# Four DMA transposes of an encoder kernel replaced by TensorE transposes into PSUM

## The chip, the cores and the metric

The kernel runs on one core of one Trainium2 chip. The metric is the time of one execution in device microseconds (us). The engines are TensorE (PE, with its weight loads PEld), VectorE (DVE), ScalarE (ACT), GpSimd (POOL) and SyncE (SP, which issues most of the transfers).

## The reference, cut to what matters

One encoder layer is applied to two requests (prompt and sample) of 2048 tokens and 1024 features each, with the same weights. Four groups of 256 features are computed side by side, each is multiplied by its own gate, and the concatenation goes through an output projection:

```python
hx = rms_norm(x, pre_g)
proj = hx @ w_in                                     # 1024 -> 12 * 256 + 16 columns
y_a = fourier_mix(a_u, w_fnet) * silu(a_z)           # FNet
y_b = gdn_branch(b_qkv, b_gates, ...) * silu(b_z)    # gated delta rule, both directions
y_c = neighbourhood_attn(cq, ck, cv, rpb) * silu(c_z)
y_d = memory_attn(d_q, rms_norm(mem, mem_g), w_mem_kv) * silu(d_z)
out = concatenate([y_a, y_b, y_c, y_d], -1) @ w_out
return x + rms_norm(out, post_g)
# gdn_branch: q, k, v = split(silu(centred_dwconv(qkv, conv_w)))   5 taps, 4 heads of 64
#   then per chunk of 64 tokens: a triangular solve, and a scan over 32 chunks:
v_new = u_i - w_i @ state
o = qd_i @ state + qk_i @ v_new
state = state * gl_i + kd_i.T @ v_new
# neighbourhood_attn: 32 x 64 grid of tokens, 8 x 16 keys each, softmax with a bias table
# memory_attn: 256 memory tokens, 4 heads, softmax
```

## The kernel before, in words

All large products are made from fp16 parts: a float32 value is split into a high half (the value rounded to fp16) and a low half (the rest), and three matmuls per product stand at lines L464 to L466, L474 to L476 and L480 to L482 (`mm_feat`, `mm_tok`, `mm3`). An operand with tokens on the partitions must be transposed where the features or keys are summed over, and this happens in four places by a DMA on SP's queue:

- `xblock` (L428): 256 rows of x are normalized, split (L446 on ACT, L213 on DVE: tile `xh`) and transposed to `xT` (L448), 16 blocks of 128x128 per instruction. It runs 36 times in `pass_a`, memory tokens included; a copy of `xT` is stored as `xTd` (L531), which the later passes load.
- `conv_pair` and `gdn_conv` (L857, L928): convolution and SiLU of q, k and v of 256 tokens by features, tile `cacc`. v is split into `vt` (L878 on ACT, L227 on POOL) and transposed to `vr` (L937), 16 times.
- `mem_attn.scores` (L1407): the probabilities of 128 tokens over 4 heads and 256 memory tokens are split to `mP` (L1434 on DVE, L227 on POOL) and transposed to `mPT` (L1437), 32 times.
- `na_attn.scores` (L1515): for a pair of tiles of queries the scores `nS` are made (L1561), the probabilities are put into padded tiles `np` as fp16 parts (L1578 on ACT, L1579 on DVE) and transposed to `nPT` (L1582), 64 times.

The stages are traced in this order. `pass_a` projects q, k, v and the gates of the delta rule (a block of 256 tokens at a time); `pass_b` and `pass_z` project what the other groups and the output gates need. `gdn_pre` prepares the delta rule by blocks of 256 tokens (its products are the tiles `lt` and `mt`, L990). `gdn_sub` solves the triangular systems. `gdn_chain` is the scan: 32 steps for each of the two requests, each step one state `S` (L1188 to L1194) that the next step needs. `fnet`, `mem_attn` and `na_attn` (NA) are the other groups. `pass_o` is the output projection of 16 blocks of 256 tokens, each in four quarters of 48 matmuls (`po`, L738 and following) with an `oo` (L748) each; the scale of a block's fp16 parts takes the largest value of a tile through DRAM and back (L331 and L333, tile `p2d`; DVE waits for it in L334).

What sets the order is a scheduler that orders each engine's instructions by a simulated timeline when the kernel is built. Every stage has a band of priorities, lower first: projections and `pass_o` 0, `gdn_sub` and `gdn_chain` 1 (loading a step's operands 1.5), FNet, memory attention and NA 2, `gdn_pre` 3, and the matmuls of the projections 5, so that they fill what the others leave free. Memory orders more: the pools of the left stack are opened one after the other (FNet, memory attention, NA, then the pool of `pass_o`), and those of the right stack too (`gdn_pre`, `gdn_sub`, `gdn_chain`). The PSUM pool `pat` has three tags, `s`, `t` and `o`, with one buffer each (`PSS = ("s", "t")`, `PSV = ("o", "o")`); FNet, memory attention and NA use them in turn, and `pass_o` uses `t`.

## Time and profile before

| | |
|---|---|
| time, median of 3 runs | 2710.26 us (2707.71 to 2711.54) |
| span of the profiled execution | 2710.9 us |
| instructions | 60616 |
| PE busy | 2054.5 us (76%) |
| DVE busy | 2015.0 us (74%) |
| POOL busy | 1130.4 us (42%) |
| ACT busy | 1047.5 us (39%) |
| DMA | 478.35 MB, mean 176 GB/s |

The profile shows one execution. The span is the time from its first to its last instruction on the chip; the profiled execution has no other time of its own on record, and its span lies within the range of the timed runs. Busy time is summed over the span, register and semaphore instructions are left out. The views used below are the page's chain (followed back from the last instruction to what released each step), busy time by window with the granted TensorE clock as a share of full speed, instructions by source line, the timeline of an engine, and waits.

### The profile page before, as it was taken

The page shows a single profiled execution, that of the slowest core. Times are in us where ns is not written, and L with a number is a line of the kernel's source. Part 1 is how long each engine was busy: PE and PEld are TensorE (multiplying, and loading weights), DVE is VectorE, ACT ScalarE, POOL GpSimd, SP SyncE. Part 2 cuts the span into 40 slices and gives each one's busy share as a digit, 9 for nine tenths or more (in the row PEclk, how much of TensorE's full clock was granted, in tenths as well). Part 3 has the DMA queues.
Part 4 walks back from the last instruction along what each step waited for, and adds up shares of the span by engine and source line. Part 5 has one row for each costly group of instructions (what it writes and reads, how often), then busy time and mean ns, then how long its engine had stood idle before and what let it go on. Part 6 is the DMA issues. An engine that isn't in the chain of part 4 may idle for free.

```text
span 2710.9 us, 60616 instructions
## 1 busy us (share of the span) xinstructions
PE 2054.5 (76%) x23664; PEld 1730.0 (64%) x23664; DVE 2015.0 (74%) x4958; ACT 1047.5 (39%) x2544; POOL 1130.4 (42%) x1275
## 2 busy tenths in 40 slices
PE   0676787777667777997589988777788687787778
PEld 0465666666446666775467777667677576676667
DVE  2369988989899979479758758867766567766654
ACT  1345446443454322342254526555542332222221
POOL 1126646455576676427565242222223434433320
PEclk9888888898779898998789989999999888889989
DMA  9799899999956693899489979999997556566443
GB/s 76 150 195 204 192 221 238 213 201 216 171 137 174 200 179 89 202 197 147 114 162 187 186 206 213 204 202 200 192 203 238 141 166 182 142 174 172 142 120 109
DMA packets 834976, 478.35 MB, mean 176 GB/s; under 512 B 562048, under 2 KB 795392, under 8 KB 826240
## 3 DMA queue, kind: packets, MB, share of 16 engines
q1 hardware_dynamic: 810112, 440.92, 76.1%
q10 hardware_dynamic: 24576, 33.56, 4.3%
q8 instruction: 185, 3.03, 0.5%
q14 instruction: 103, 0.84, 0.1%
HBM read 245.60 MB, written 163.75 MB: 151 GB/s over the span
## 4 chain that ended last, share of the span: by engine, by line
DVE 35%; DMA 32%; PE 16%; issue 6%; POOL 4%; SPq 3%; ACT 3%; ACTq 0%; DVEq 0%; POOLq 0%
DMA p2d<-ty 7%; DVE cacc L868 5%; DMA ty<-p2d 3%; DMA nPT<-np__3176_28761 3%; PE pj L464 3%; PE pj L465 3%; PE pj L466 3%; DMA xT<-xh 2%; DMA nPT<-np__3178_28765 2%; DVE pr L1033 2%; DVE T L1036 2%; DMA nPT<-np__3175_28759 1%; DVE ty L243 1%; DMA L<-lt 1%; DVE ty L244 1%
## 5 line engine op out<-in xcount | busy, mean ns | idle before, releaser
L464 PE MATMUL pj<-xT,w 128*128 128x256 f16 x2592 | 744.7, 287 | 140.2 <-DMA xT<-xh 62.7
L466 PE MATMUL pj<-xT,w 128*128 128x256 f16 x2592 | 743.2, 287 | 4.6 <-POOL w L401 4.6
L465 PE MATMUL pj<-xT,w 128*128 128x256 f16 x2592 | 744.2, 287 | 0.0
L464 PEld LDWEIGHTS <-w 128*128 128x128 f16 x2592 | 266.6, 103 | 129.0 <-issue 70.9
L465 PEld LDWEIGHTS <-w 128*128 128x128 f16 x2592 | 266.2, 103 | 104.8 <-issue 62.6
L480 PE MATMUL po<-w,oy 128*128 128x256 f16 x1024 | 292.3, 285 | 15.9 <-DVE oo L748 8.8
L466 PEld LDWEIGHTS <-w 128*128 128x128 f16 x2592 | 266.9, 103 | 56.0 <-issue 6.7
L481 PE MATMUL po<-w,oy 128*128 128x256 f16 x1024 | 292.7, 286 | 0.3 <-issue 0.3
L482 PE MATMUL po<-w,oy 128*128 128x256 f16 x1024 | 292.4, 286 | 0.0
L868 DVE SCALAR_TENSOR_TENSOR cacc<-craw,cws,cacc 128x256 f32<-128x256 f32 x384 | 236.1, 650 | 9.5 <-ACT cacc L866 8.8
L474 PE MATMUL pj<-w,xT 128*128 128x272 f16 (+1 forms) x512 | 153.2, 300 | 50.1 <-ACT st L541 30.6
L475 PE MATMUL pj<-w,xT 128*128 128x272 f16 (+1 forms) x512 | 153.0, 299 | 5.8 <-POOL w L401 5.8
L401 POOL TENSOR_TENSOR w<-wt,w 128x512 f16<-128x512 f32 (+1 forms) x70 | 87.7, 1261 | 161.6 <-ACT w L399 130.9
L476 PE MATMUL pj<-w,xT 128*128 128x272 f16 (+1 forms) x512 | 152.5, 298 | 0.0
L227 POOL TENSOR_TENSOR km<-kt,km 128x256 f16<-128x256 f32 x128 | 105.5, 848 | 110.1 <-ACT km L986 108.6
L1128 POOL COPY bk<-rA 64x512 f16<-64x512 f16 x124 | 79.8, 644 | 159.1 <-DMA rA<-recs 119.0
L480 PEld LDWEIGHTS <-b 128*128 128x128 f16 x1008 | 98.3, 102 | 71.6 <-DVE ct L1179 32.1
L334 DVE TENSOR_REDUCE ty<-ty 128x1 f32<-128x128 f32 x34 | 9.6, 283 | 180.7 <-DMA ty<-p2d 180.7
L227 POOL TENSOR_TENSOR mP<-mP,mP 128x1024 f16<-128x1024 f32 x32 | 68.4, 2137 | 176.7 <-DVE ty L1450 107.7
L1138 POOL COPY b<-cT 64x256 f16<-64x256 f16 x128 | 60.5, 472 | 169.9 <-PE pc L482 161.1
L480 PE MATMUL pno<-nPT,nv 128*128 128x64 f16 x704 | 78.7, 200 | 62.0 <-DMA nPT<-np__3176_28761 24.9
L481 PEld LDWEIGHTS <-oy 128*128 128x128 f16 x1024 | 104.9, 102 | 32.0 <-issue 16.6
(431 smaller groups left out, 6751.0 us busy)
## 6 DMA issues: line engine op xcount, KB each, us to landing
xT<-xTd SPq DMA_DIRECT2D x32, 1024.0 KB
rec<-km SPq DMA_DIRECT2D x32, 768.0 KB
rA<-rec SPq DMA_DIRECT2D x64, 384.0 KB
xTd<-xT SPq DMA_DIRECT2D x16, 1024.0 KB
sz<-st ACTq DMA_DIRECT2D x64, 256.0 KB
oz<-sz SPq DMA_DIRECT2D x16, 1024.0 KB
out_dram<-oo SPq DMA_DIRECT2D x32, 512.0 KB
craw<-braw SPq DMA_DIRECT2D x48, 260.0 KB
```

What stands on the lines that cost most here:

```text
L227: self.nc.gpsimd.tensor_tensor(out=out, in0=a, in1=b, op=ALU.subtract)
L401: eng.tensor_tensor(out=w[:, kk, 1, :], in0=t, in1=w[:, kk, 0, :], op=ALU.subtract)
L464: nc.tensor.matmul(ps, whi, xhi, start=(kt == 0), stop=False)
L465: nc.tensor.matmul(ps, whi, xlo, start=False, stop=False)
L466: nc.tensor.matmul(ps, wlo, xhi, start=False, stop=(kt == KT - 1))
L474: nc.tensor.matmul(ps, xhi, whi, start=(kt == 0), stop=False)
L475: nc.tensor.matmul(ps, xhi, wlo, start=False, stop=False)
L476: nc.tensor.matmul(ps, xlo, whi, start=False, stop=(kt == KT - 1))
L480: nc.tensor.matmul(ps, whi, xhi, start=start, stop=False)
L481: nc.tensor.matmul(ps, whi, xlo, start=False, stop=False)
L482: nc.tensor.matmul(ps, wlo, xhi, start=False, stop=stop)
L868: nc.vector.scalar_tensor_tensor(out=acc[:, f], in0=raw[:, f, t:t + CB], scalar=w[:, t:t + 1], in1=acc[:, f], op0=ALU.mult, op1=ALU.add)
```

## The change

The four DMA transposes are taken out. In their places each 128x128 block is transposed by TensorE (a matmul with an identity) into a tile of `pat`. In `xblock` the two fp16 halves are transposed as they are (eight blocks each, tags `s` and `t`) and copied by ACT to `xT`. In the other three the float32 values are transposed, and the split is made from PSUM: ACT copies the high half to fp16 and DVE subtracts it for the low half. The convolution of v is written to `cacc` in the order of chunks, so that a block of 128 columns holds both feature halves of 64 tokens. NA's padded tiles become float32 without halves, its scores use tag `s` alone (they used `s` and `t` in turn) and its transposes tag `t`. The rest of the diff removes comments and is not shown.

```diff
@@ -445,7 +445,11 @@
...
             self.split_lo(nc.vector, hl[:, 1], xts[t], hl[:, 0], rs[:, t:t + 1])
-            nc.sync.dma_start(dst[:, :, :, t * P:t * P + P].rearrange("p l k t -> p (l k) t"), hl.rearrange("p l c -> p (l c)"), transpose=True)
+            for l in range(2):
+                pt = self.pat.tile([P, KT, P], F16, name=self.nm("pxt"), tag=PSS[l])
+                for k in range(KT):
+                    nc.tensor.transpose(pt[:, k], hl[:, l, k * P:k * P + P], self.ident16)
+                nc.scalar.activation(dst[:, l, :, t * P:t * P + P], pt, AF.Copy)
             self.pace = hl[:, 1, 0:1]
@@ -855,35 +859,45 @@
...
         nc.sync.dma_start(raw, self.D[f"braw{r}"][:, 2 * i:2 * i + 2, tb * CB:tb * CB + CB + 4])
-        acc = pp.tile([P, 2, CB], F32, name=self.nm("cacc"), tag="cacc", bufs=2)
+        acc = pp.tile([P, 2 * CB], F32, name=self.nm("cacc"), tag="cacc", bufs=2)
+        ch = lambda t: t.rearrange("p (n c) -> p n c", c=64)
+        if u == "v":
+            af = [acc.rearrange("p (n f c) -> p f n c", f=2, c=64)[:, f] for f in range(2)]
+        else:
+            af = [ch(acc[:, f * CB:f * CB + CB]) for f in range(2)]
         for f in range(2):
             w = self.cws[:, 2 * i + f]
-            nc.scalar.activation(acc[:, f], raw[:, f, 0:CB], AF.Copy, scale=w[:, 0:1])
+            nc.scalar.activation(af[f], ch(raw[:, f, 0:CB]), AF.Copy, scale=w[:, 0:1])
             for t in range(1, 5):
-                nc.vector.scalar_tensor_tensor(out=acc[:, f], in0=raw[:, f, t:t + CB], scalar=w[:, t:t + 1], in1=acc[:, f], op0=ALU.mult, op1=ALU.add)
-        e = pp.tile([P, 2, CB], F32, name=self.nm("cexp"), tag="cexp", bufs=2)
+                nc.vector.scalar_tensor_tensor(out=af[f], in0=ch(raw[:, f, t:t + CB]), scalar=w[:, t:t + 1], in1=af[f], op0=ALU.mult, op1=ALU.add)
+        e = pp.tile([P, 2 * CB], F32, name=self.nm("cexp"), tag="cexp", bufs=2)
         nc.scalar.activation(e, acc, AF.Tanh, scale=self.cinv[:, i:i + 1])
...
         if u == "v":
-            dst = [self.vt[:, :, l].rearrange("p n f c -> p f n c") for l in range(2)]
+            pv = self.pat.tile([P, CB // 64, P], F32, name=self.nm("pvt"), tag=PSV[0])
+            for n in range(CB // 64):
+                nc.tensor.transpose(pv[:, n], acc[:, n * P:n * P + P], self.ident)
+            nc.scalar.activation(self.vr[:, :, 0], pv, AF.Copy)
+            nc.vector.tensor_tensor(out=self.vr[:, :, 1], in0=pv, in1=self.vr[:, :, 0], op=ALU.subtract)
         else:
+            ac = acc.rearrange("p (f n c) -> p f n c", f=2, c=64)
             kind = 0 if u == "k" else 1
             dst = [self.kq[:, :, kind, :, l].rearrange("p n f c -> p f n c") for l in range(2)]
-        ac = acc.rearrange("p f (n c) -> p f n c", c=64)
-        nc.scalar.activation(dst[0], ac, AF.Copy)
-        self.gsub(dst[1], ac, dst[0])
-        if u != "v":
+            nc.scalar.activation(dst[0], ac, AF.Copy)
+            self.gsub(dst[1], ac, dst[0])
             nc.scalar.activation(e, acc, AF.Square)
-            ep = self.tops(nc.gpsimd, e, pp.tile([P, 2, CB], F32, name=self.nm("csq"), tag="csq"))
+            ep = self.tops(nc.gpsimd, e, pp.tile([P, 2 * CB], F32, name=self.nm("csq"), tag="csq"))
             for t in range(CB // P):
...
                     for k in range(3):
-                        nc.tensor.matmul(self.pss[:, t, 2 * i + f], ep[k][:, f, t * P:t * P + P], self.onesbd[:, 0:P:64], start=(k == 0), stop=(k == 2))
+                        nc.tensor.matmul(self.pss[:, t, 2 * i + f], ep[k][:, f * CB + t * P:f * CB + t * P + P], self.onesbd[:, 0:P:64], start=(k == 0), stop=(k == 2))
 
@@ -928,20 +942,17 @@
...
         self.kq = kq.bitcast(F16).rearrange("p n (k f l c) -> p n k f l c", k=2, f=2, l=2)
-        self.vt = pp.tile([P, CB // 64, 2, 2, 64], F16, name=self.nm("vt"), tag="vt", bufs=2)
+        self.vr = vr = pp.tile([P, CB // 64, 2, P], F16, name=self.nm("vr"), tag="vr", bufs=2)
         self.pss = self.pgd.tile([P, CB // P, 4, 2], F32, name=self.nm("pss"), tag="as")
...
             self.conv_pair(r, pp, tb, u)
-        vr = pp.tile([P, CB // 64, 256], F16, name=self.nm("vr"), tag="vr", bufs=1)
-        self.nc.sync.dma_start(vr.rearrange("p n (x c) -> p (n x) c", c=P), self.vt.rearrange("p n l f c -> p (n l f c)"), transpose=True)
-        self.nc.sync.dma_start(self.D[f"recs{r}"][4 * tb:4 * tb + 4, :, 0:128].rearrange("n p x -> p n x"), vr.bitcast(F32))
+        self.nc.sync.dma_start(self.D[f"recs{r}"][4 * tb:4 * tb + 4, :, 0:128].rearrange("n p x -> p n x"), vr.rearrange("p n l x -> p n (l x)").bitcast(F32))
         self.nc.sync.dma_start(self.D[f"recs{r}"][4 * tb:4 * tb + 4, :, 128:256].rearrange("n p x -> p n x"), kq[:, :, 128:256])
@@ -1425,16 +1436,19 @@
...
                         nc.scalar.activation(Pf[:, k], ps[:, h], AF.Exp, scale=dS[:, 0:1], bias=mx[:, 0, k:k + 1], accum_out=mx[:, 1, k:k + 1])
-                P16 = T([P, 2, 4, 256], F16, "mP16", 3)
-                nc.vector.tensor_copy(P16[:, 0], Pf)
-                self.gsub(P16[:, 1], Pf, P16[:, 0])
                 PT = T([P, 2, 8, P], F16, "mPT", 3)
-                nc.sync.dma_start(PT.rearrange("p l x t -> p (l x) t"), P16.rearrange("p l h m -> p (l h m)"), transpose=True)
+                for hp in range(2):
+                    pt = self.pat.tile([P, 4, P], F32, name=self.nm("pmt"), tag=PSS[hp])
+                    for x in range(4):
+                        nc.tensor.transpose(pt[:, x], Pf[:, 2 * hp + x // 2, (x % 2) * P:(x % 2) * P + P], self.ident)
+                    xs = slice(4 * hp, 4 * hp + 4)
+                    nc.scalar.activation(PT[:, 0, xs], pt, AF.Copy)
+                    nc.vector.tensor_tensor(out=PT[:, 1, xs], in0=pt, in1=PT[:, 0, xs], op=ALU.subtract)
                 return PT, mx, v16
@@ -1460,16 +1474,16 @@
...
             nxt = scores(*todo[0])
-            self.na_setup(lambda: T([P, 2, 4, 256], F16, "mP16", 3).rearrange("p l h m -> p (l h m)").bitcast(F32))
+            self.na_setup(lambda: T([P, 2, 8, P], F16, "mPT", 3).rearrange("p l x t -> p (l x t)").bitcast(F32))
             for j, ri in enumerate(todo):
@@ -1492,8 +1506,8 @@
...
             qb, = self.bds(mp, "nqb", [P, 2, 2, 8, 2, 32], F16, 1, nc.vector)
-            self.npad = [self.bds(mp, f"np{k}_", [P, 2, 2, 12, 32], F16, n, nc.vector) for k, n in enumerate((1, 2, 1))]
+            self.npad = [self.bds(mp, f"np{k}_", [P, 2, 12, 32], F32, n, nc.vector) for k, n in enumerate((1, 2, 1))]
             kr = mp.tile([P, 2, 2, 16, 64], F16, name="nkr", tag="nkr")
@@ -1538,12 +1552,12 @@
...
                     rows.append((16 - r0, 0, nr - 16 + r0))
-                ps = self.pat.tile([P, 2, 253], F32, name=self.nm("pns"), tag=PSS[p % 2])
+                ps = self.pat.tile([P, 2, 253], F32, name=self.nm("pns"), tag=PSS[0])
                 sm = self.tt([P, 4, 2], tag="nsm")
@@ -1567,19 +1581,19 @@
...
                 pads = self.npad[(p + 1) // 2][p == 2]
+                PT = T([P, 2, 2, 3, P], F16, "nPT", 2)
                 for x in range(2):
                     S, n, nk, ci, off, _ = out[x]
-                    pad = pads[:, x]
                     Sv = S[:, 0:n].rearrange("p (r c) -> p r c", c=nk)
-                    hi = pad[:, 0, 0:nr, off:off + nk]
-                    lo = pad[:, 1, 0:nr, off:off + nk]
-                    nc.scalar.activation(hi, Sv, AF.Copy, scale=sm[:, 3, x:x + 1])
-                    nc.vector.scalar_tensor_tensor(out=lo, in0=Sv, scalar=sm[:, 3, x:x + 1], in1=hi, op0=ALU.mult, op1=ALU.subtract)
+                    nc.scalar.activation(pads[:, x, 0:nr, off:off + nk], Sv, AF.Copy, scale=sm[:, 3, x:x + 1])
+                    pt = self.pat.tile([P, 3, P], F32, name=self.nm("pnt"), tag=PSS[1])
+                    for g in range(ng):
+                        nc.tensor.transpose(pt[:, g], pads[:, x, 4 * g:4 * g + 4].rearrange("p r c -> p (r c)"), self.ident)
+                    nc.scalar.activation(PT[:, x, 0, 0:ng], pt[:, 0:ng], AF.Copy)
+                    nc.vector.tensor_tensor(out=PT[:, x, 1, 0:ng], in0=pt[:, 0:ng], in1=PT[:, x, 0, 0:ng], op=ALU.subtract)
                     res.append(ci)
-                PT = T([P, 2, 2, 3, P], F16, "nPT", 2)
-                nc.sync.dma_start(PT.rearrange("p x l g t -> p (x l g) t"), pads.rearrange("p x l r c -> p (x l r c)"), transpose=True)
                 return PT, res
```

The order of the instructions is made anew with it. On DVE in `pass_a`, in the projection of the second request, the low halves of the 25th and 26th of the 36 tiles of x (`xh`, L213) are followed by this before (`lt` and `mt` are the delta rule's products, `cacc` its convolution):

```order
L213 SCALAR_TENSOR_TENSOR xh_3710<-xt_3686,ty_3695,xh_3710 128x1024
L213 SCALAR_TENSOR_TENSOR xh_3714<-xt_3690,ty_3695,xh_3714 128x1024
L990 TENSOR_TENSOR lt_14194<-p_1235_14196,df_14189 128x2x128
L990 TENSOR_TENSOR mt_14213<-p_1235_14196,df_14189 128x256
L990 TENSOR_TENSOR lt_14194<-p_1238_14219,df_14189 128x2x128
L990 TENSOR_TENSOR mt_14236<-p_1238_14219,df_14189 128x256
L868 SCALAR_TENSOR_TENSOR cacc_14139<-craw_14137,cws,cacc_14139 128x256 x4
L868 SCALAR_TENSOR_TENSOR cacc_14309<-craw_14307,cws,cacc_14309 128x256
L868 SCALAR_TENSOR_TENSOR cacc_14139<-craw_14137,cws,cacc_14139 128x256 x2
L868 SCALAR_TENSOR_TENSOR cacc_14309<-craw_14307,cws,cacc_14309 128x256
```

And after, around the 26th and the 27th (`gw`, `gam`, `ke` and `beta` belong to the delta rule's gates):

```order
L213 SCALAR_TENSOR_TENSOR xh_4189<-xt_4146,ty_4151,xh_4189 128x1024
L811 TENSOR_TENSOR gw_3419<-gw_3419,expal 128x32
L814 TENSOR_SCALAR beta_951<-gw_3422 128x4x8
L221 TENSOR_TENSOR gw_3426<-gw_3419 128x32
L223 TENSOR_TENSOR gw_3426<-gw_3426 128x32
L213 SCALAR_TENSOR_TENSOR xh_4451<-xt_4427,ty_4436,xh_4451 128x1024
L823 COPY gam_954<-pga_3425 128x4x8
L830 TENSOR_SCALAR ke_953<-ke_953 128x4x8
```

The chunk products and convolutions that stood right behind the x blocks are not there; gates are.

On DVE in the scan of the second request, one step stands so before (`S` the state, `ot` and `b` of the step, `oo` and `oy` of the output projection):

```order
L1188 SCALAR_TENSOR_TENSOR S_23700<-pc_23687,sd_23701 128x256
L1201 TENSOR_TENSOR ot_23720<-pc_23707,ct_23685 128x256
L1139 COPY b_1714_18282<-rA_23723 64x24x64 x2
L1194 TENSOR_TENSOR S_2420_23704<-S_23700,S_2420_23704 128x256
L748 TENSOR_TENSOR oo_34064<-po_34228,gpost 128x512
L720 TENSOR_REDUCE ty_34065<-ty_34063 128x2
L721 TENSOR_SCALAR ty_34065<-ty_34065,ty_33752 128x2
L239 TENSOR_SCALAR ty_34283<-ty_34065 128x2
L240 TENSOR_SCALAR ty_34283<-ty_34283 128x2
L243 SCALAR_TENSOR_TENSOR ty_34284<-ty_34283 128x2
L697 SCALAR_TENSOR_TENSOR oy_3714_34301<-oy_34031,ty_34051,oy_3714_34301 128x2048
```

And after (line numbers are up to 14 higher; `nPT` and `pnt` are the new transposes of NA, `nS` its scores):

```order
L1199 SCALAR_TENSOR_TENSOR S_23760<-pc_23747,sd_23761 128x256
L1595 TENSOR_TENSOR nPT_32550<-pnt_32552,nPT_32550 128x256
L1582 TENSOR_SCALAR ty_32895<-ty_32895 128x2
L1212 TENSOR_TENSOR ot_23780<-pc_23767,ct_23745 128x256
L1150 COPY b_1786_19014<-rA_23783 64x24x64 x2
L1575 ISA nS_32981,ty_32974<-pns_32973,natab 128x176
L1575 ISA ty_32974 128x1
L1205 TENSOR_TENSOR S_2408_23764<-S_23760,S_2408_23764 128x256
L1595 TENSOR_TENSOR nPT_32550<-pnt_32558,nPT_32550 128x256
```

The step's own instructions are the same; the output projection's beside it have given place to NA's.

## Rows read from the trace of the kernel before

**Rows 1.** The page, its section 4: chain that ended last, by engine and by line.
```profile
DVE 35%; DMA 32%; PE 16%; issue 6%; POOL 4%; SPq 3%; ACT 3%; ACTq 0%; DVEq 0%; POOLq 0%
DMA p2d<-ty 7%; DVE cacc L868 5%; DMA ty<-p2d 3%; DMA nPT<-np__3176_28761 3%; PE pj L464 3%; PE pj L465 3%; PE pj L466 3%; DMA xT<-xh 2%; DMA nPT<-np__3178_28765 2%; DVE pr L1033 2%; DVE T L1036 2%; DMA nPT<-np__3175_28759 1%; DVE ty L243 1%; DMA L<-lt 1%; DVE ty L244 1%
```

**Rows 2.** Busy us by window: length, PE, PEld, DVE, ACT, POOL, clock, DMA share, GB/s.
```profile
0.00:80.00 80.00, 1.96 (x7) 1.24 (x8) 20.00 (x58) 11.51 (x19) 9.80 (x15) 1.00 1.06 77
80.00:705.00 625.00, 465.16 (x4157) 383.43 (x4158) 526.27 (x1347) 287.58 (x625) 305.92 (x309) 0.86 0.99 205
705.00:965.00 260.00, 184.04 (x1657) 152.11 (x1657) 249.49 (x559) 114.40 (x259) 164.53 (x169) 0.85 0.64 166
965.00:1591.00 626.00, 515.13 (x5242) 415.56 (x5240) 458.54 (x771) 220.73 (x513) 329.73 (x361) 0.89 0.82 166
1591.00:2566.00 975.00, 774.83 (x11581) 678.95 (x11579) 690.05 (x2029) 381.47 (x1036) 303.05 (x411) 0.91 0.79 186
2566.00:2711.00 145.00, 113.38 (x1028) 98.67 (x1026) 70.69 (x197) 31.83 (x94) 17.35 (x12) 0.90 0.37 107
```

**Rows 3.** Timeline of SP's queue at the start: start us, us, line, op.
```profile
42.17 35.64 SPq L448 DMA_TRANSPOSE xT<-xh  x2
77.90 2.36 SPq L368 DMA_DIRECT2D w<-in_w_in_dram  x3
```

**Rows 4.** Ends of stages by line: ns min/median/max, first and last start us.
```profile
L549 DVE TENSOR_SCALAR gates<-pj,wsc_ag x32: 213/224/234, 118.7 to 705.5; 128x16 f32<-128x16 f32 x32
L990 DVE TENSOR_TENSOR lt<-p,df x64: 402/410/425, 230.2 to 965.1; 128x256 f32<-128x256 f32 x64
L1194 DVE TENSOR_TENSOR S<-S,S x62: 404/420/1443, 1590.7 to 2566.1; 128x256 f16<-128x256 f32 x62
```

**Rows 5.** Timeline of PE near 2146 us: start us, us, line, op, count.
```profile
2146.35 0.27 PE L466 MATMUL pj<-xT,w 128*128 128x256 f16 x1
2146.46 0.60 PE L681 MATMUL pot<-ident,oyb 128*128 128x128 f32 x4
2146.90 0.27 PE L464 MATMUL pj<-xT,w 128*128 128x256 f16 x1
```

**Rows 6.** Durations by line of the nearest operations: ns min/median/max.
```profile
L446 ACT ACTIVATE xh<-xt,ty x36: 1132/1138/1151, 13.1 to 600.4; 128x1024 f16<-128x1024 f32 x36
L878 ACT ACTIVATE vt<-cacc x16: 612/630/631, 175.6 to 905.9; 128x512 f16<-128x512 f32 x16
L1427 DVE TENSOR_REDUCE ty<-pms x64: 628/680/692, 1148.3 to 1559.3; 128x2 f32<-128x512 f32 x64
L1434 DVE CAST mP<-mP x32: 671/693/2621, 1152.7 to 1561.6; 128x1024 f16<-128x1024 f32 x32
L227 POOL TENSOR_TENSOR mP<-mP,mP x32: 2118/2126/2386, 1153.5 to 1574.9; 128x1024 f16<-128x1024 f32 x32
L1579 DVE SCALAR_TENSOR_TENSOR np__3176_28761<-nS,ty,np__3176_28761 x32: 404/479/954, 1629.5 to 1998.2; 128x253 f16<-128x253 f32 x24, 128x184 f16<-128x184 f32 x8
```

**Rows 7.** SP's transposes by line, and who waited for those of nPT.
```profile
L448 SPq DMA_TRANSPOSE xT<-xh x36: 1322/3886/19364, 42.2 to 620.1; - x36
L1437 SPq DMA_TRANSPOSE mPT<-mP x32: 1879/3020/6702, 1157.7 to 1577.0; - x32
L1582 SPq DMA_TRANSPOSE nPT<-np__3176_28761 x16: 1434/3128/7509, 1638.1 to 2004.0; - x16
  PE pno L480: 56.7, 28
```

**Rows 8.** Waits in 2150:2605: engine, line, waited for, us in total, times, longest.
```profile
ACT S L1193 <- DVE S L1188: 93.3, 19, 11.5
DVE ty L334 <- DMA ty<-p2d: 84.7, 13, 9.0
```

**Rows 9.** Busy us in the NA stretch and in the out-projection's, columns as Rows 2.
```profile
1630.00:2018.00 388.00, 312.08 (x5874) 274.49 (x5870) 290.50 (x1075) 219.22 (x628) 88.41 (x151) 0.93 1.05 203
2150.00:2605.00 455.00, 356.92 (x4154) 309.79 (x4150) 319.30 (x757) 121.92 (x325) 172.90 (x193) 0.89 0.58 162
```

## The prediction

> **What bounds the kernel now.** I read the page's chain first [rows 1]: no engine owns the end. DVE has 35% of the chain, transfers 32%, PE 16%. Two of the four transposes stand in it by name, nPT (3% and 2% for two of its four pads) and xT (2%). So no single duration decides, and the next view is the busy time by stage [rows 2]. Its five cuts are ends of work: the first projection matmul (80), the end of pass_a (705), of the delta rule's preparation (965), the first step of the scan (1591) and the last (2566) [rows 4]. DVE is busy 84% in pass_a (526.27 of 625), 96% in the rest of the preparation (249.49 of 260), 73% from there to the scan (458.54 of 626), 71% during the scan (690.05 of 975) and 49% in the tail (70.69 of 145). PE is under 83% in every stage. The kernel is thus DVE's list of work, stretched by waits, with a tail in which DVE waits on round trips. The reader should look at which work stands beside the scan: in the kernel before it is NA, the last gate projections and 43 of the 64 quarters of the out-projection; 21 quarters remain for the tail.
>
> **The parts, by their own work.** PE gets 576 fp16 and 672 float32 transposes. Four float32 ones took the place of 0.44 us between two matmuls whose neighbours are 0.11 apart [rows 5], so 672 x 0.11 = 74 us; the fp16 ones are not in the trace: at least nothing (hidden), at most the same 0.11, and I take half of it, since the matmul of 256 columns takes 0.11 for twice the columns: 576 x 0.06 = 35 us. ACT gets 72 copies of 128x1024 (1.138 each from the nearest row, L446), 64 of 128x512 and 128 of about 128x350: 82 + 64 x 0.630 (L878) + 128 x 0.45 (as L1579, below) = 180 us [rows 6], on an engine that is idle over half the time. DVE loses 32 casts (L1434, 0.693) and 128 subtractions (L1579: 0.479 in its larger form, 0.45 taken for the mean), 80 us, and gets 64 subtractions from PSUM of 128x512 (L1427 reads such a tile in 0.680), 128 smaller and 16 for the values: 44 + 61 + 11 = 116 us. That is +36 us in a list of 2015 (the sum of [rows 2]). POOL loses 32 x 2.126 = 68 us [rows 6] and 16 smaller pieces. SP loses 36 + 32 + 64 transposes of 3.9, 3.0 and about 2.9 us at the median [rows 7], and 16 of the values' size.
>
> By themselves, then, the edits give transfers and SP back and take 36 us of DVE. On the trace's 3.020 us for the 16 blocks of one mPT transpose a block costs 0.19 us of queue, against 0.11 of PE and a share of two copies. The Trainium skill (VectorE: DVE Perf Modes, section on the three transpose paths) gives 390 ns on TensorE and 1309 ns by DMA for a 128x128 block, both far above these rows; by its figures the transfers given back would weigh more than three times what is put on PE. The measured ones say that the two are near each other, and I go by them.
>
> **What the change moves.** The order of each engine is made anew, and it differs far from the edits. I priced every DVE row of both orders at the mean time of its group in the trace. For the order before this reproduces the stages: 802 us of DVE work up to the last lt, 1254 to the first scan step, 1958 to the last, as the sums of [rows 2] do (796, 1254, 1944). For the order after it gives 803, 1221 and 1864. What stands there differs: ahead of the last pass_a gates 8 of the 64 chunks of the preparation in place of 40, and at the first scan step 16 of the 32 memory items in place of 31, but 48 of 64 gate quarters in place of 23. At the last scan step only 5 of the 64 out-projection quarters are done in place of 43, because NA (which must close before the out-projection's tiles exist) now ends at scan step 54 of 62 in place of 28.
>
> Stage by stage:
> - A, end of pass_a. Without the chunks it is bound by PE: 3264 matmuls of 256 columns and 576 transposes ahead of its end are 3264 x 0.11 + 35 = 394 us at full clock, 458 at the 0.86 granted there [rows 2]. The start is earlier: the first two transposes held SP for 35.64 us from 42.17 with the weights' load behind them [rows 3]. Without them I put the first matmul near 62. So A = 62 + 458 = 520, bounds 471 (full clock, and 77 us of start) to 592 (PE at the 74% that [rows 2] show, 465.16 of 625, for the 394 us). Before: 705.
> - B, last chunk. 320 us of DVE work are done by 520, 483 remain; at the 96% of that stage before, 503 us: B = 1023. Before: 965. The gain of A is given back, since the chunks that ran in its gaps come after it.
> - C, first scan step. 1221 - 803 = 418 us of DVE at the 73% of that stage: 572, so 1595. Before: 1591.
> - D, 61 scan steps. 1864 - 1221 = 643 us of DVE. The share is the choice here. The NA stretch ran at 75% (290.50 of 388), the out-projection stretch at 70%, but with 84.7 us of its 455 spent in L334's wait for the largest value that goes through DRAM [rows 8, 9], so 86% of the rest. NA moves beside more scan steps and that wait leaves the scan with the out-projection. I take the middle, 81%: 794 us, to 2389. Bounds: 96% (the best stage) 670, 71% (now) 906.
> - E, the tail. 59 quarters remain in place of 21, that is 14.75 blocks of four in place of 5.25. The tail took 145 us for 5.25 blocks, 27.6 each, of which 48 x 4 matmuls at 0.11 are 21 on PE. L334's waits stand in it, up to 9.0 us each before its start [rows 8]. A longer tail has less start and end in it; I take 25.5, 376 us. Bounds: 21 (PE alone) 310, 27.6: 407.
>
> Sum 2389 + 376 = 2765 us, +2.0%. The profiled execution's span, 2710.9, is within 0.03% of the median of the runs, 2710.26, so nothing is added around it. The cover that makes the edits cheap is the scan: its steps wait on their own chain (93 us of ACT's wait for S in the out-projection stretch is part of that chain [rows 8]), and NA fills this. If NA did not, D would be at its upper bound.
>
> **What is queued behind the new waits.** In NA the pair of tiles goes through one PSUM buffer: transposes, ACT's copy, DVE's subtraction, then the next tile's transposes. DVE's subtraction stands in order between scan steps (the second place shown of the order), so a late ACT copy holds the scan's S behind it. The next tile's transposes wait on PE for that subtraction, with the scan's matmuls behind them.
>
> **Rivals.**
> - R1, faster by the transfers. In NA the DMA engines' share is 1.05 [rows 9], PE's pno waited 56.7 us for nPT [rows 7]; the chain has xT and nPT in it [rows 1]. If transfers are what stretches DVE's list, stages C and D go at 87% in place of 73 and 81: 480 + 739 + 1023 + 376 = 2618 us. Against: the out-projection stretch has a DMA share of 0.58 and its DVE share is no higher than in NA with 1.05 [rows 9], so it is not the transfers that stretch DVE there. Chance 0.30.
> - R2, slower by NA's round trips. If each of 128 tiles has its round trip in series (0.44 for the transposes, 0.45 for ACT and 0.45 for DVE, from [rows 5, 6]; 1.3 us, 170 us in all) and the scan does not cover it, the time is 2765 + 170 = 2935. It decides once the items of NA, not the scan's own chain, set the pace of D; before, 64 items took 388 us [rows 9], 6.1 each, for 25 scan steps, so there is a margin. Chance 0.12.
> - R3, no difference: D at 86% (748) gives 2719, and a little less in E gives 2710. Chance 0.05 within 0.2%, about 5.4 us, which is what a measurement of this kernel can tell from no change.
> - That DMA transposes remain is excluded: the order after has none in SP's list.
>
> The Trainium skill (Advanced Engine Details and Errata, section X-Bar Transpose (TRN2)) says that transposing DMAs are as fast as regular ones. By that rule R1 would lose its ground. The trace disagrees in part: SP's L448 has a median of 3.886 us and a longest of 19.364 [rows 7].
>
> **How the numbers follow.** Forecast 0.53 with its own range 2680 to 2870 (D at 71% to 91%, mostly), R1 0.30, R2 0.12, R3 0.05. All of the forecast's range but its low end is slower, and R2 is; R1 and that end are faster: faster 0.33, same 0.05, slower 0.62. The range that leaves 2 in 10 out goes from 2595 (somewhat under R1, whose share could be a little over 87%) to 2890 (above D's upper bound with the forecast's tail, 2877, below R2).
>
> **What would show it right or wrong.** In the changed profile: the last gates near 520, the last lt near 1023, the first S near 1595, the last S near 2390 and a tail near 375 us that is PE at 80% and L334 waits. The step on which most hangs is D: if DVE is over 87% busy between the first and the last S, R1 holds; under 72% with waits of PE or DVE on pnt and nPT, R2. If the tail goes in under 21 us a block, or if the out-projection is found beside the scan after all, E is wrong.

## The result, and the profile after

The changed kernel takes 2872.03 us in the median (2870.69 to 2874.33), the kernel before in the same comparison 2708.99: a ratio of 1.062, interval 1.059 to 1.065. It is slower by 163 us, where 55 were forecast. The profiled execution took 2871.41 us and its span is 2869.6, so the stages below add up to the time within 2 us.

The chain that ended last, from the page of the changed kernel, answers to [rows 1]:

```profile
DVE 19%; PE 16%; DMA 14%; POOL 4%; issue 3%; ACT 2%; SPq 2%; POOLq 0%; DVEq 0%; ACTq 0%
DMA p2d<-ty 6%; DMA ty<-p2d 3%; DVE pr L1044 2%; PE pj L470 2%; PE pj L469 2%; PE pj L468 2%; DVE T L1047 2%; POOL oy L230 2%; DVE b L1150 2%; DVE ty L692 1%; DVE oy L701 1%; DMA oy<-ya 1%; DVE nPT L1595 1%; PE pc L485 1%; PE pmt L1448 1%
```

The transposes by DMA are gone from the entries shown, and so is `cacc`; the round trip `p2d` is the first entry, as before. It covers only 60% of the span, so the busy time by stage says more. Its columns are those of [rows 2], the cuts again the ends of pass_a, of the preparation, and the first and last step of the scan:

```profile
0.00:80.00 80.00, 14.92 (x86) 10.53 (x86) 17.12 (x56) 15.70 (x23) 6.39 (x12) 0.73 0.94 91
80.00:624.00 544.00, 440.86 (x4083) 375.97 (x4084) 264.30 (x812) 253.12 (x463) 90.91 (x89) 0.90 0.51 135
624.00:1191.00 567.00, 428.60 (x3991) 359.70 (x3991) 528.04 (x1081) 237.93 (x534) 355.84 (x381) 0.90 0.57 159
1191.00:1711.00 520.00, 416.56 (x4338) 346.84 (x4337) 387.36 (x725) 192.46 (x393) 268.29 (x325) 0.90 0.72 155
1711.00:2453.00 742.00, 558.27 (x9575) 478.24 (x9573) 599.83 (x1879) 408.85 (x1137) 238.39 (x374) 0.87 0.49 143
2453.00:2870.00 417.00, 335.44 (x2846) 288.46 (x2843) 203.93 (x458) 93.15 (x261) 72.37 (x47) 0.90 0.39 135
```

And the rows that give the cuts, as in [rows 4], with `oo` for the out-projection:

```profile
L553 DVE TENSOR_SCALAR gates<-pj,wsc_ag x32: 221/233/235, 138.3 to 624.1; 128x16 f32<-128x16 f32 x32
L1001 DVE TENSOR_TENSOR lt<-p,df x64: 406/412/426, 223.5 to 1191.3; 128x256 f32<-128x256 f32 x64
L1205 DVE TENSOR_TENSOR S<-S,S x62: 404/421/1168, 1710.9 to 2452.6; 128x256 f16<-128x256 f32 x62
L752 DVE TENSOR_TENSOR oo<-po,gpost x64: 675/684/692, 2405.1 to 2861.2; 128x512 f32<-128x512 f32 x64
```

The reader sees three things. The second stage has DVE busy 264 us of 544, 49%, where before it was 84%: pass_a is shorter (624 in place of 705), but the chunks that filled it are not there. The preparation ends at 1191 in place of 965, and the scan begins 120 us later. Then the scan is much shorter, 742 us in place of 975, with its last step at 2453, 113 us earlier than before; but the out-projection, which began at 2159 and stood beside the scan, begins at 2405 and has 417 us of the tail to itself.

What holds the chunks back stands in no list of waits, since the order of the engines was made with it. It is seen when the last and the first use of one PSUM buffer, tag `o`, are laid side by side: the gates' last tile (`pgt`), v's transposes (`pvt`) and FNet's products (`pfy`), each with its first and last start. The fourth line has the chunks (`lt`) that were done by 624 us, the time of the last gates:

```profile
L832 PE MATMUL pgt<-ident,gam x8: 272/273/395, 207.3 to 650.1; 128*32 128x128 f32 x8
L886 PE MATMUL pvt<-ident,cacc x64: 272/273/474, 655.9 to 1142.1; 128*128 128x128 f32 x64
L484 PE MATMUL pfy<-ph,fw16s x96: 216/270/417, 1146.8 to 1448.9; 128*128 128x128 f16 x48, 128*128 128x256 f16 x48
L1001 DVE TENSOR_TENSOR lt<-p,df x8: 406/416/425, 223.5 to 262.8; 128x256 f32<-128x256 f32 x8
```

The last `pgt` of pass_a is at 650.1, the first `pvt` at 655.9; the last `pvt` is at 1142.1, the first `pfy` at 1146.8. The buffer is handed from one to the next in the order in which the stages are written, and all of pass_a is written ahead of `gdn_pre`, and that ahead of FNet. The changed kernel put v into that queue: a convolution block whose operands are there in the first 200 us cannot pass on its v until pass_a's last gates are done. Two blocks (8 chunks) went ahead, the last of them at 262.8, and then the preparation stood still. The kernel before had this queue too, with FNet right behind the gates:

```profile
791.77 0.27 PE L828 MATMUL pgt<-ident,gam 128*32 128x128 f32 x1
799.53 0.27 PE L480 MATMUL pfy<-ph,fw16s 128*128 128x128 f16 x1 [0.71 <-DVE gT L830]
```

FNet's first product came 8 us after the gates' last tile, released by DVE's copy of it (`gT`). Now FNet's products come 347 us later, and memory attention and NA come behind FNet.

### The profile page after: what moved, and what is told of

The parts are those of the page before. It is cut to its first block, busy times and chain, and to the rows that moved or that the text cites. A ratio compares the mean times of both kernels' runs of the same rounds, so it can differ in the third digit from the quotient of the medians.

```text
span 2869.6 us, 63126 instructions
## 1 busy us (share of the span) xinstructions
PE 2194.6 (76%) x24912; PEld 1859.7 (65%) x24912; DVE 2000.6 (70%) x5006; ACT 1201.2 (42%) x2808; POOL 1032.2 (36%) x1227
## 4 chain that ended last, share of the span: by engine, by line
DVE 19%; PE 16%; DMA 14%; POOL 4%; issue 3%; ACT 2%; SPq 2%; POOLq 0%; DVEq 0%; ACTq 0%
DMA p2d<-ty 6%; DMA ty<-p2d 3%; DVE pr L1044 2%; PE pj L470 2%; PE pj L469 2%; PE pj L468 2%; DVE T L1047 2%; POOL oy L230 2%; DVE b L1150 2%; DVE ty L692 1%; DVE oy L701 1%; DMA oy<-ya 1%; DVE nPT L1595 1%; PE pc L485 1%; PE pmt L1448 1%
## 5 line engine op out<-in xcount | busy, mean ns | idle before, releaser
L468 PE MATMUL pj<-xT,w 128*128 128x256 f16 x2592 | 733.1, 283 | 83.7 <-DVE st L649 36.6
L470 PE MATMUL pj<-xT,w 128*128 128x256 f16 x2592 | 732.2, 282 | 15.5 <-DVE w L401 14.0
L469 PE MATMUL pj<-xT,w 128*128 128x256 f16 x2592 | 732.5, 283 | 1.9 <-ACT xT L452 1.9
L469 PEld LDWEIGHTS <-w 128*128 128x128 f16 x2592 | 262.6, 101 | 95.9 <-issue 59.0
L468 PEld LDWEIGHTS <-w 128*128 128x128 f16 x2592 | 263.0, 101 | 67.0 <-DMA xT<-xTd 18.3
L470 PEld LDWEIGHTS <-w 128*128 128x128 f16 x2592 | 262.9, 101 | 58.4 <-DVE w L401 14.5
L878 DVE SCALAR_TENSOR_TENSOR cacc<-craw,cws,cacc 128x256 f32<-128x256 f32 x384 | 268.2, 738 | 1.9 <-ACT cacc L876 1.0
L478 PE MATMUL pj<-w,xT 128*128 128x272 f16 (+1 forms) x512 | 156.8, 307 | 67.7 <-DVE st L213 30.8
L230 POOL TENSOR_TENSOR oy<-oy,oz 128x512 f32<-128x512 f32 x60 | 90.1, 1520 | 246.4 <-ACT oy L686 220.7
L485 PEld LDWEIGHTS <-oy 128*128 128x128 f16 x1024 | 105.5, 103 | 93.9 <-issue 76.8
L750 ACT ACTIVATE oj<-po,wsc_o 128x256 f32<-128x256 f32 x128 | 59.4, 468 | 235.8 <-PE po L486 235.7
L479 PE MATMUL pj<-w,xT 128*128 128x272 f16 (+1 forms) x512 | 157.0, 307 | 0.9 <-POOL w L401 0.9
L480 PE MATMUL pj<-w,xT 128*128 128x272 f16 (+1 forms) x512 | 156.4, 306 | 0.0
L485 PEld LDWEIGHTS <-b 128*128 128x128 f16 x1008 | 96.7, 104 | 46.9 <-issue 46.3
L484 PEld LDWEIGHTS <-b 128*128 128x128 f16 x1008 | 99.8, 104 | 36.7 <-DVE og L1225 16.4
L486 PEld LDWEIGHTS <-oy 128*128 128x128 f16 x1024 | 105.7, 103 | 19.1 <-DVE oy L701 1.8
```

Of the source, the lines that this page charges most:

```text
L230: self.nc.gpsimd.tensor_tensor(out=out, in0=a, in1=b, op=ALU.mult)
L468: nc.tensor.matmul(ps, whi, xhi, start=(kt == 0), stop=False)
L469: nc.tensor.matmul(ps, whi, xlo, start=False, stop=False)
L470: nc.tensor.matmul(ps, wlo, xhi, start=False, stop=(kt == KT - 1))
L478: nc.tensor.matmul(ps, xhi, whi, start=(kt == 0), stop=False)
L479: nc.tensor.matmul(ps, xhi, wlo, start=False, stop=False)
```

## The experiments

Each run is compared with the kernel before on the same chip: time in us, ratio, and the ratio's interval in brackets. The edits are cut to the lines that tell, and "..." marks a cut. Theory P and rival N are named in the first expectation, rival D in that of e5.

**e1, v alone.** Of the change only the part of v:

```diff
...
-        self.vt = pp.tile([P, CB // 64, 2, 2, 64], F16, name=self.nm("vt"), tag="vt", bufs=2)
...
+            pv = self.pat.tile([P, CB // 64, P], F32, name=self.nm("pvt"), tag=PSV[0])
```

> The kernel before with the change of v alone (transposes of v by TensorE into the tag o of the PSUM pool). Theory P (a place in a PSUM queue): the first transpose of v stands behind the last gate tile of pass_a in the one buffer of tag o, so the delta rule's preparation stops at 8 chunks until pass_a ends, as in the changed kernel (first transpose of v at 656 us, 6 us after the last gate tile's transpose at 650). It expects the first transpose of v only after the last gates, the last chunk at 1100 or later in place of 965, and 2770 to 2850 us. Rival N (NA's round trips and the out-projection that comes late behind them cost the time): 2690 to 2730 us here, since NA is as before.

Measured 2892.88 us, 1.066 [1.063, 1.070], more than the whole change and above the range that P expected. Its last gate tile, its transposes of v and its scan:

```profile
L828 PE MATMUL pgt<-ident,gam x8: 272/273/285, 183.9 to 632.4; 128*32 128x128 f32 x8
L882 PE MATMUL pvt<-ident,cacc x64: 272/273/476, 643.7 to 1133.7; 128*128 128x128 f32 x64
L1201 DVE TENSOR_TENSOR S<-S,S x62: 393/417/1956, 1769.4 to 2745.0; 128x256 f16<-128x256 f32 x62
```

The first transpose of v is 11 us behind the last gate tile, the first scan step 179 us later than in [rows 4], and so is the last (2745.0 against 2566.1); the end is 178 us later (2889.1 against 2710.9). Rival N, by which v is harmless, falls.

**e2, the change without v.** From the changed kernel, v's part undone:

```diff
...
-            pv = self.pat.tile([P, CB // 64, P], F32, name=self.nm("pvt"), tag=PSV[0])
...
+        self.vt = pp.tile([P, CB // 64, 2, 2, 64], F16, name=self.nm("vt"), tag="vt", bufs=2)
```

> The changed kernel with the part of v undone (v split first and transposed by DMA, as before); x, memory attention and NA by TensorE. Theory P: 40 or more chunks go beside pass_a again, the last chunk at 900 to 980 us, and 2690 to 2770 us in all. Rival N: within 30 us of the changed kernel's 2872.

Measured 2721.20, 1.003 [1.002, 1.005], with 48 chunks ahead of the last gates (767) and the last chunk at 935, as theory P has it:

```profile
L994 DVE TENSOR_TENSOR lt<-p,df x64: 400/412/426, 226.7 to 935.0; 128x256 f32<-128x256 f32 x64
```

**e3, v on TensorE in another buffer.** All four transposes as in the change, but v's go to the buffer that the preparation itself uses, after its norms:

```diff
...
+        self.norms(r, pp, tb)
...
+        pv = self.pgd.tile([P, CB // 64, P], F32, name=self.nm("pvt"), tag="as")
```

> The changed kernel with all four transposes on TensorE, but the transposed v in tag as of the preparation's own PSUM pool, after the norms, in place of tag o. Theory P: the same as the run without v within 30 us (2690 to 2780), with the first transpose of v near 170 us in place of 656. If it were the work of the transposes of v and not its place in the queue: 2840 to 2880. Rival N: 2840 to 2880 too.

Measured 2741.93, 1.012 [1.009, 1.016].

```profile
L949 PE MATMUL pvt<-ident,cacc x64: 272/273/387, 201.1 to 905.7; 128*128 128x128 f32 x64
L1207 DVE TENSOR_TENSOR S<-S,S x62: 403/418/855, 1485.4 to 2189.7; 128x256 f16<-128x256 f32 x62
```

The same 64 transposes begin at 201 in place of 656, and the scan at 1485 in place of 1711. 130 us of the 163 go with the tag; what is left, 33 us, is the change in all four places. The part of v, in a buffer of its own, costs the 21 us between this run and e2.

**e9, the gates out of tag o.** The changed kernel with v in `o` and the gates' two tiles in the projections' buffers:

```diff
...
-        ps = self.pat.tile([P, 3, 4 * n], F32, name=self.nm("pga"), tag="o")
+        ps = self.pmm.tile([P, 3, 4 * n], F32, name=self.nm("pga"), tag="mm")
...
-        pt = self.pat.tile([4 * n, P], F32, name=self.nm("pgt"), tag="o")
+        pt = self.pmm.tile([4 * n, P], F32, name=self.nm("pgt"), tag="mm")
```

> The changed kernel with all its transposes as they are, v in tag o too, but the tiles of the delta rule's gates (pga and pgt, two places) taken from tag o to the projections' own PSUM buffers. Theory P: the wait of the first transpose of v goes (it starts near 200 us in place of 656), the last chunk comes at 900 to 990, FNet's products in tag o still start only after the last transpose of v, 2700 to 2790 us in all. If it were not the gates ahead of it in tag o but v's transposes sharing any buffer with FNet: 2830 to 2900.

Measured 2855.58, 1.055 [1.053, 1.058]: a miss for the time that P expected.

```profile
L553 DVE TENSOR_SCALAR gates<-pj,wsc_ag x32: 219/226/234, 138.5 to 933.7; 128x16 f32<-128x16 f32 x32
L886 PE MATMUL pvt<-ident,cacc x64: 272/375/476, 198.1 to 998.3; 128*128 128x128 f32 x64
```

The wait is gone (198 in place of 656) and the first scan step came at 1541 in place of 1711, but pass_a's last gates are at 934 in place of 624 and the last chunk at 1034, where 900 to 990 was expected: the gates' tiles now stood in the queue of the projections, and these came late (last gate projection 2354 against 1906). The time lies in the range of the other view, by which v costs by sharing any buffer with FNet. But the run moved the queue instead of removing it, so it settles nothing between the two. Hence the next run:

**e12, the gates in tag s.** v alone, in `o`, with the gates' tiles in a tag that nothing else of pass_a uses:

```diff
...
-        ps = self.pat.tile([P, 3, 4 * n], F32, name=self.nm("pga"), tag="o")
+        ps = self.pat.tile([P, 3, 4 * n], F32, name=self.nm("pga"), tag="s")
...
-        pt = self.pat.tile([4 * n, P], F32, name=self.nm("pgt"), tag="o")
+        pt = self.pat.tile([4 * n, P], F32, name=self.nm("pgt"), tag="s")
```

> The change of v alone with v in tag o as in the changed kernel, but the gates' tiles in tag s, which nothing else uses in pass_a of this kernel. It leaves the projections' buffers alone, as the run with the gates there did not. Theory P: the first transpose of v near 200 us, the last chunk at 940 to 1000, the first scan step at 1560 to 1640 in place of 1769, 2700 to 2770 us in place of 2893. If v in tag o costs by sharing it with FNet, whose products stay behind the last transpose of v: over 2800.

Measured 2747.83, 1.015 [1.009, 1.021], 145 us less than e1.

```profile
L882 PE MATMUL pvt<-ident,cacc x64: 272/273/474, 170.6 to 891.9; 128*128 128x128 f32 x64
L1201 DVE TENSOR_TENSOR S<-S,S x62: 394/421/1265, 1536.1 to 2478.6; 128x256 f16<-128x256 f32 x62
```

Nothing of v or of its place in `o` was touched, only what stands ahead of it there. The numbers are about where P had them (the first transpose 171, the last chunk 931, the first step 1536, each a little earlier than expected). FNet's products still stand behind v's last transpose (904 after 892), so sharing with FNet is not what cost these 145 us. The place behind the gates is shown to be the cause of them, out of the 182 that v alone cost. The 38 us that are left over the kernel before are not taken apart; about 20 are what v's part costs in a buffer of its own (e2 and e3).

**e4, x alone; e5, NA alone; e6, memory attention alone.**

```diff
...
+                pt = self.pat.tile([P, KT, P], F16, name=self.nm("pxt"), tag=PSS[l])
```
```diff
...
+                    pt = self.pat.tile([P, 3, P], F32, name=self.nm("pnt"), tag=PSS[1])
```
```diff
...
+                    pt = self.pat.tile([P, 4, P], F32, name=self.nm("pmt"), tag=PSS[hp])
```

> The kernel before with the change of x alone. Theory P: the DMA transposes of x and the 36 us that the first two held SP are gone, nothing is put behind the gates: 2640 to 2700 us, the first projection matmul near 20 us. Rival N also expects no loss here, 2640 to 2720; a third view, that the transposes' and ACT's copies in pass_a hold PE and ACT, expects 2720 to 2760.

> The kernel before with the change of NA alone (transposes by TensorE through one buffer of tag t, scores through one of tag s). Theory P (the loss is the place of v in the PSUM queue; the other parts give nothing back because NA and the projections end late and the out-projection then runs without cover): NA ends some 100 to 200 us later than at 2000, 10 to 25 quarters of the out-projection are done at the last scan step in place of 43, 2715 to 2790 us. Rival D (the DMA transposes of NA were in the way): NA shorter than 380 us and 2640 to 2700.

> The kernel before with the change of memory attention alone. Theory P: nothing is queued anew ahead of the scan, some out-projection loses its cover: 2700 to 2750 us. Rival D: POOL's 68 us and SP's 97 us of transposes are given back, 2640 to 2700.

Measured for x 2740.10, 1.011 [1.007, 1.015]; for NA 2721.54, 1.006 [1.004, 1.009]; for memory attention 2674.83, 0.989 [0.986, 0.992].

With x alone the first projection matmul is as early as expected (19 us), but the kernel ends 29 us later than before, a miss for P and inside the third view's range: pass_a ended at 766 in place of 705, with ACT busy 390 us up to there where it had been 299 up to 705. The scan began 37 us earlier (1554), while the last gate projection, at lower priority, came at 2221 in place of 2150, and the out-projection behind it at 2239. No run tells whether ACT's copies are the cause.

With NA alone, NA ended at 2162 in place of 2000 and 11 quarters were done at the last scan step, inside what P expected; D's gain is not there. Its scores took 540 us from the first to the last in place of 380, with PE busy 484 of them and the whole scan 752 us in place of 975. In the changed kernel, where the last gate projection (1906) came before NA's first score (1919), they took 390. So the length of NA went with what stood beside it; what its round trips cost by themselves is not separated.

Memory attention is where D is right: it is the one part that gains. Of the kernel before, POOL's waits between 965 and 1600 us, its splits of the probabilities up to 1434, and its share of the triangular solve (`pr`):

```profile
POOL mP L227 <- DVE ty L1450: 107.7, 17, 23.6
POOL mP L227 <- DVE mP L1434: 40.4, 5, 15.2
L227 POOL TENSOR_TENSOR mP<-mP,mP 128x1024 f16<-128x1024 f32 x19 | 40.8, 2145 | 102.7 <-DVE ty L1450 60.3 <-DVE mP L1434 25.5 <-ACT zb L1084 8.4
L1033 POOL TENSOR_TENSOR pr<-A,T x124: 227/592/2172, 985.0 to 1434.4; 128x31 f32<-128x31 f32 x8, 128x60 f32<-128x60 f32 x8, 128x87 f32<-128x87 f32 x8, 128x112 f32<-128x112 f32 x8
```

And in e6 the solve, and the scan:

```profile
L1033 POOL TENSOR_TENSOR pr<-A,T x124: 228/598/2173, 970.1 to 1346.0; 128x31 f32<-128x31 f32 x8, 128x60 f32<-128x60 f32 x8, 128x87 f32<-128x87 f32 x8, 128x112 f32<-128x112 f32 x8
L1194 DVE TENSOR_TENSOR S<-S,S x62: 393/421/1479, 1483.4 to 2401.7; 128x256 f16<-128x256 f32 x62
```

In POOL's list the splits of the probabilities (`mP`) stood among the solve's products. Before, they waited 148 us for DVE, 86 of them (60.3 and 25.5) ahead of the solve's last product, and were busy 41 us there. Without them the solve ends at 1346 in place of 1434 and the scan begins at 1483 in place of 1591. That this is where the gain comes from is argued from these waits: e6 also takes away DVE's casts and SP's transposes, and no run parts them. With 2674.83 us e6 is faster than both kernels and the best of these runs.

**e10, memory attention and v in its own buffer** (e6 and e3's edit of v).

```diff
...
+                    pt = self.pat.tile([P, 4, P], F32, name=self.nm("pmt"), tag=PSS[hp])
...
+        pv = self.pgd.tile([P, CB // 64, P], F32, name=self.nm("pvt"), tag="as")
```

> The kernel before with the changes of memory attention and of v, v in tag as after the norms; x and NA by DMA as before. Theory P with each part's own worth: memory attention gave 2675, v in its own queue takes 16 casts' subtractions from POOL and puts 11 us on DVE: 2655 to 2695. Rival (v by TensorE costs by itself, as the 20 us between the run with v in tag as and the run without v): 2690 to 2710.

Measured 2693.59, 0.994 [0.992, 0.996], where the two ranges overlap. It is 19 us more than e6, close to the 21 between e2 and e3, which speaks for the rival.

**e7, e8, e11 and e13, other priorities.** In this order: x alone, the change without v, and memory attention twice. `CHAIN` is the band of the scan, `ASM` that of the loading of its operands, `GEMM_PE` that of the projections' matmuls, and `scan` in the last edit that of `gdn_pre`. The other lines of each edit are those of e4, e2 and e6:

```diff
-ASM = 1.5
-CHAIN = 1
+ASM = 2.6
+CHAIN = 2.5
```
```diff
-GEMM_PE = 5
+GEMM_PE = 2.5
```
```diff
-ASM = 1.5
-CHAIN = 1
+ASM = 2.6
+CHAIN = 2.5
```
```diff
-GEMM_PE = 5
-ASM = 1.5
-CHAIN = 1
+GEMM_PE = 2.2
+ASM = 2.6
+CHAIN = 2.5
...
-        gemm, scan, mix = 0, 3, 2
+        gemm, scan, mix = 0, 2.1, 2
```

> The change of x alone, with the scan put behind memory attention and NA in priority (its band 1 made 2.5, and the loading of its operands 2.6 in place of 1.5). Theory P: NA ends early, the out-projection begins before 2200 us and stands beside the scan again; 2660 to 2730 against 2740 with the bands as they were. A rival (the projections, not NA, hold the out-projection back: the last gate projection was at 2221 us): the out-projection does not begin before 2200, and the time is 2720 to 2780.

> The changed kernel without v, and with the projections' matmuls ahead of the delta rule's preparation in priority (band 2.5 in place of 5; order after: 8 chunks beside pass_a, all gate projections and memory items before the scan). Theory P with cover: the last gate projection comes before 1900 us, the out-projection begins in the scan, but the scan begins 100 us or more later: 2620 to 2760. Rival (late chunks alone make it slow, as with v in tag o): 2800 to 2900.

> Memory attention's change alone, with the scan behind memory attention and NA in priority (bands 2.5 and 2.6). If the cover of the out-projection by the scan were what is short (27 quarters done at the last scan step in place of 43): 2630 to 2670, with 41 quarters done. If the out-projection's beginning (last gate projection at 2148) decides: within 20 us of 2675, or more, as the scan ends later.

> Memory attention's change alone with other bands: preparation 2.1, projections' matmuls 2.2, scan 2.5, loading of its operands 2.6, so that the projections go ahead of the scan (order: all gate projections before the first scan step, NA before it too, 48 quarters of the out-projection beside the scan). In the runs so far the time from the first quarter to the end was 450 us plus 2.3 for each quarter that stood beside the scan, and the first quarter came 5 to 100 us after the later of the last gate projection and NA's end. If that beginning decides, it comes before 2000 us and the time is 2500 to 2640. If the scan's own length decides (62 steps of 12 us at the least, from a first step at 1900 or later): 2680 to 2800.

Measured for e7 2757.85, 1.020 [1.017, 1.022]; e8 3243.29, 1.199 [1.195, 1.202]; e11 2704.28, 0.998 [0.995, 1.001]; e13 3074.37, 1.135 [1.131, 1.140]. e7 and e11 went as their rivals said: NA ended early (1906 and 1920), but the gate projections did not, and more cover brought nothing. e8 was far worse than either view expected, with the last chunk at 1894. e13 began the out-projection at 2202, not before 2000, and its scan, from 2004 to 2910, set the end; it was slower than the second view expected too. So the beginning of the out-projection decides only while the scan is out of the way.

What the other runs have in common is in this table, by the traces: the last gate projection, NA's end (its last scores), the first quarter of the out-projection, the quarters done at the last scan step, and the time from the first quarter to the end.

| kernel | last gate projection | NA's end | first quarter | beside the scan | first quarter to end |
|---|---|---|---|---|---|
| before | 2150 | 2000 | 2159 | 43 | 552 |
| after | 1906 | 2308 | 2405 | 5 | 465 |
| e1 | 1884 | 2268 | 2351 | 42 | 538 |
| e2 | 2200 | 2123 | 2257 | 0 | 451 |
| e3 | 2191 | 2200 | 2284 | 0 | 450 |
| e4 | 2221 | 1968 | 2239 | 25 | 493 |
| e5 | 2108 | 2162 | 2251 | 11 | 474 |
| e6 | 2148 | 1974 | 2157 | 27 | 510 |
| e7 | 2207 | 1906 | 2211 | 38 | 544 |
| e9 | 2354 | 2268 | 2390 | 0 | 455 |
| e10 | 2185 | 1976 | 2194 | 23 | 501 |
| e11 | 2131 | 1920 | 2138 | 41 | 551 |
| e12 | 2232 | 2018 | 2238 | 25 | 509 |

The out-projection begins 4 to 97 us after the later of the two, and then takes 450 us by itself and about 2.4 more for each quarter beside the scan ((552 - 450) / 43; the other rows come within 16 us of that). In the changed kernel NA is the later one, at 2308: it stands at the end of the queue from the gates through v, FNet and memory attention.

## Why the prediction was wrong, point by point

The direction was right, the size was not, and the cause was not seen. The order was read rightly: 8 chunks ahead of the last gates, 16 memory items and 48 gate quarters at the first scan step, 5 quarters at the last one, all as in the trace. The prediction priced the new order and did not ask why it was so. The chunks had left pass_a because of a place in a PSUM queue, and no rival named that. The step that failed is the price of A and B, the stages that this queue stretched: 168 us too little. E was 41 us too little as well. That C and D came out 104 us shorter than priced hid part of this, which was luck.

- **A failed.** "Bound by PE: 3264 x 0.11 + 35", with the end at 520 and at most 592; it was 624. PE was busy 441 us of the 544 after 80 us, near the 458 of the sum, but not without gaps: the sum had no idle time in it, and 103 us of it were measured, in many short waits. The first 80 us, although the first projection matmul came at 20 and not at 62, had only 15 us of PE work. The longest waits of PE from 80 to 624, then two of the longest in the first 80, for x and for its squares:

```profile
PE pj L478 <- ACT st L545: 27.4, 6, 13.0
PE pxt L451 <- DVE xh L213: 13.3, 1, 13.3
ACT xq L438 <- DMA xt<-in_x_prompt_dram: 57.5, 5, 33.2
DVE ty L440 <- ACT xq L438: 38.8, 1, 38.8
```

- **B** had the rate right (528.04 of 567, 93%, against 96%), but 281 us of DVE work were done by the end of pass_a in place of 320, and A's delay stood ahead of it: 1191 in place of 1023. A and B together are 168 us too little.
- **C** took 520 us in place of 572, at 74% (387.36 of 520) against 73%: the rate was right, the work 31 us less than priced.
- **D** took 742 us in place of 794. The share that was chosen between 75 and 86%, 81%, is what was measured (599.83 of 742); the work was 600 in place of 643. R1 has no support here, with DVE under the 87% that it wanted: the DMA share of NA fell from 1.05 [rows 9] to 0.49, and DVE rose to 89% there, but NA took 388 us as before:

```profile
1920.00:2308.00 388.00, 287.66 (x5681) 249.64 (x5679) 343.73 (x1248) 263.43 (x752) 121.19 (x202) 0.88 0.49 139
```

- R2's single buffer is seen, but small: PE's transposes waited for DVE's subtraction 28.5 us in all, over 42 times, and the weight loads of these transposes 35.2 over 40, where R2 had 170 us of round trips:

```profile
  PEld pnt L1593: 35.2, 40
  PE pnt L1593: 28.5, 42
```

- **E** took 417 us in place of 376, that is 28.3 a block of four where 25.5 was taken; the 27.6 of the tail before would have given 407. From the first quarter to the end, ACT's squares waited for the matmuls, and DVE for the largest value, now up to 14.4 us each:

```profile
ACT oj L750 <- PE po L486: 235.7, 60, 11.1
DVE ty L334 <- DMA ty<-p2d: 165.1, 14, 14.4
```

Sum of the misses: +168 - 52 - 52 + 41 = 105, and 2765 + 105 = 2870. The terms for the edits themselves were small and near, as the new lines show against [rows 6]:

```profile
L452 ACT ACTIVATE xT<-pxt x72: 998/1018/1088, 16.4 to 543.9; 128x1024 f16<-128x1024 f16 x72
L451 PE MATMUL pxt<-ident,xh x576: 216/219/315, 14.5 to 543.3; 128*128 128x128 f16 x192
305.34 0.61 PE L451 MATMUL pxt<-ident,xh 128*128 128x128 f16 x8
305.79 0.27 PE L470 MATMUL pj<-xT,w 128*128 128x256 f16 x1
L1450 ACT ACTIVATE mPT<-pmt x64: 569/597/619, 1485.7 to 1898.8; 128x512 f16<-128x512 f32 x64
L1451 DVE TENSOR_TENSOR mPT<-pmt,mPT x64: 669/682/693, 1486.3 to 1899.9; 128x512 f16<-128x512 f32 x64
L1595 DVE TENSOR_TENSOR nPT<-pnt,nPT x128: 397/546/559, 1933.7 to 2334.2; 128x384 f16<-128x384 f32 x96, 128x256 f16<-128x256 f32 x32
```

ACT's copies of x took 1.018 (1.138 forecast), DVE's subtractions 0.682 and 0.546 (0.680 and 0.48), and an fp16 transpose is half of a float32 one in the spacing, as was guessed: the next matmul starts 0.45 us after the first of eight, so 0.06 each. DVE's list did not grow by 36 us but shrank by 14, to 2000.6. The largest single saving is told at the end.

The figures of the Trainium skill (VectorE: DVE Perf Modes, section The three transpose paths), 390 ns on TensorE and 1309 ns by DMA for a 128x128 block of bf16, make TensorE's path the shorter one. In these traces a block in a row takes far less on either path, 0.06 (fp16) or 0.11 us (float32) on TensorE and 0.19 by DMA, so the order of the two is the same. But the copies out of PSUM come on top, 0.13 us a block on ACT for x (1.018 for eight), and all four transposes on TensorE with the queue taken away (e3) cost 33 us more than by DMA, the new order included.

The prediction set the length of SP's transposes against a rule on regular transfers with no such transfer of the same data beside it. What the trace compares is how long SP was held: 3.886 us at the median by a transpose of x [rows 7], 0.328 by a store of `xT` (L531). What the transfers themselves took is not compared.

## What to carry to other kernels

Where a change adds a tile to a shared PSUM buffer, list the tag's users in the order in which they are written, and look in the trace of before when the last user ahead of it ends: here that was 792 us, for a transpose that used to start at 177 (L937). When a scheduler makes the order, a large shift in the order of work that was not edited can be a sign of such a queue; ask for its cause before pricing it. And a change in four places is four changes: alone, one gained 1.1%, and three lost 0.6, 1.1 and 6.6%.
